# Hybrid encoder block: the low parts of the mixed Fourier channels subtracted by GpSimd in place of VectorE

## The chip, the core and the metric

The kernel runs on one NeuronCore of a Trainium2 chip. The metric is the device time of one execution in microseconds (us), lower being better; several runs are taken, and their median counts. The engines are named as in the profile: PE (TensorE matmuls), PEld (its weight loads), DVE (VectorE), ACT (ScalarE), POOL (GpSimd), SP (the queue that issues most DMAs).

## What is computed

One layer of an encoder over 2064 tokens (2048 of the sequence and 16 learned ones in front) with 1024 channels. One projection gives queries, keys and values of an attention group (4 query heads, 2 key heads) and 512 channels of a Fourier group. The part that matters here, cut from the reference:

```python
four = fourier_mix(u, w_fourier[i])     # real part of a 2-D FFT, then a 128x128 product per group
mixed = jnp.concatenate([rms_norm(attn, g_attn_out[i]), rms_norm(four, g_fourier_out[i])], axis=-1)
h = h + mixed @ w_out[i]
m = rms_norm(h, g_mlp[i])
h = h + jnp.square(jax.nn.relu(m @ w_up[i])) @ w_down[i]
```

The Fourier half of `mixed @ w_out` is the stage that is changed: `rms_norm(four)` times the lower 512 rows of `w_out`, added to `x`.

## The kernel before

Products of float32 precision are made as three fast ones. A value `a` is split into a high part `hi` (rounded to the type `fp32r`) and a low part `lo = a - hi`, and `mm3` (lines 77 to 82) issues hi x hi, hi x lo and lo x hi into one PSUM bank: L80, L81 and L82 in the profile. The helper `Split` (line 61) makes the two parts: ACT writes `hi` (L70), DVE subtracts (L71).

The kernel goes through projection, Fourier transform, attention, the two output projections and a large feed-forward part. Attention is a generator (`attention`, line 734) that is advanced in small steps by the other stages, so that its work lies among theirs. It runs in units, one for 256 queries and one key head: for each of 16 key tiles it copies scores from PSUM (`S`, ACT), takes a running maximum (`M`, DVE L779), then, one unit later, subtracts the maximum (`S`, DVE L832), takes the exponential (ACT), sums (`acc`, DVE L839), splits the result (`ph` by ACT L70, `pl` by DVE L71) and multiplies with the values (PE, tile `o`). The buffers of `ph` and `pl` are two deep.

The stage of the change is `out_f` (line 909), for 16 tiles of 128 tokens. Its function `rows(t)` (line 916) prepares tile t: the transformed channels lie in two SBUF tensors, `EV` and `UA`, with even and odd tokens apart; for each run of such tokens (128 x 4 x 64 values, one tile has its runs in two pieces) `hi` and `lo` (`yh` and `yl`, two buffers each) are written into every second column, the square goes to `sq` (`ysq`, ACT), and POOL folds the four groups of `sq` with two additions of 256 and of 128 columns:

```python
y = src[:, :, col:col + n]
o = 2 * (e - 64 * t) + par
v = slice(o, o + 2 * n - 1, 2)
split(hi[:, :, v], lo[:, :, v], y)
nc.scalar.square(sq[:, :, v], y)
```

`scale(t)` sums `sq` over the channels on PE (`pys`), takes the mean on DVE (`ms_f`, L190), and the power -1/2 on POOL (`rs_f`, L192). The products of a tile are 24 matmuls of 128x512, 12 for each half of the output channels (bank `pof`), and DVE adds `pof * rs_f` to the tokens (`xo`, L957). `rows(t + 1)` is called while the products of tile t are issued, that is one tile ahead.

The line of code says only what is done. The order in which each engine gets its instructions is made when the program is built, by a scheduler that gives every instruction a cost and puts it where it would be ready; a change of engine in one line so moves others too. Each engine then takes its instructions strictly in that order, PE included. POOL has, besides the additions and `rs_f`, the issue of the attention's loads (`q`, `kt`, `vt`, lines 711 to 744).

Of the kernel before, what the change touches and what calls it, by code (L numbers as in the profile page):

```python
# [14 lines left out]
ALU = mybir.AluOpType  # L15
# [41 lines left out]
def f32v(ap):  # L57
    return ap.bitcast(F32)
# [18 lines left out]
def mm3(nc, out, a, b, first, last, chain=False):  # L77


    nc.tensor.matmul(out, a[0], b[0], start=first, stop=False, skip_group_check=chain)  # L80
    nc.tensor.matmul(out, a[0], b[1], start=False, stop=False, skip_group_check=chain)  # L81
    nc.tensor.matmul(out, a[1], b[0], start=False, stop=last, skip_group_check=chain)  # L82
# [53 lines left out]
def encoder_block(ctx: ExitStack, tc: tile.TileContext, x, meta, w_in, w_f,  # L136
                  w_out, w_up, w_down, g_fin, g_cols, g_rows, c_id, c_rope, c_dft, c_even, c_odd, c_rem, out):
    nc = tc.nc
    split = Split(nc)
# [9 lines left out]
    def bank(name, shape=(P, 512)):  # L149
        return mmp.tile(list(shape), F32, name=name, tag="mm")  # L150
# [36 lines left out]
    def rstd_of(pool, ss, n, width, tag, rows=P):  # L187

        ms = pool.tile([P, n], F32, name="ms_" + tag, tag="ms_" + tag, bufs=2 if pool is tp else 4)
        nc.vector.tensor_scalar(ms[:rows], ss, 1.0 / width, EPS, op0=ALU.mult, op1=ALU.add)  # L190
        rs = pool.tile([P, n], F32, name="rs_" + tag, tag="rs_" + tag, bufs=2 if pool is tp else 4)
        nc.gpsimd.tensor_tensor(rs[:rows], ms[:rows], mhalf[:rows, :n], op=ALU.pow)  # L192
        return rs
# [453 lines left out]
    def y_runs(par, e0, e1):  # L647

        m, t0, o0, t1, o1 = YO if par else YE
        got = []  # L650
        if e0 < m:
            got.append((t0, o0 + e0, e0, min(e1, m) - e0))
        if e1 > m:
            s = max(e0, m)
            got.append((t1, o1 + s - m, s, e1 - s))
        return got
# [40 lines left out]
    def misc(name, shape=(P, 512)):  # L697
        return app.tile(list(shape), F32, name=name, tag="misc")
# [204 lines left out]
    def weights(pool, bufs, k, h, keep):  # L903
        raw = pool.tile([P, 512], F32, name=f"wfr{k}_{h}", tag="wr", bufs=bufs)
        nc.sync.dma_start(raw, w_out[512 + k * P:512 + (k + 1) * P, h * 512:(h + 1) * 512])
        wt[k, h] = tuple(keep.tile([P, 512], R32, name=f"wf{e}{k}_{h}") for e in "hl")
        split(*wt[k, h], raw, c_fo(k))

    def out_f():
        xts, ops = {}, {}  # L910

        def load(t):
            xts[t] = op_.tile([P, D], F32, name=f"xo_{t}", tag="xo", bufs=2)
            nc.sync.dma_start(xts[t], x[t * P:(t + 1) * P, :])

        def rows(t):

            hi = op_.tile([P, NG, P], R32, name=f"yh_{t}", tag="yh", bufs=2)
            lo = op_.tile([P, NG, P], R32, name=f"yl_{t}", tag="yl", bufs=2)
            sq = op_.tile([P, NG, P], F32, name=f"ysq_{t}", tag="ysq", bufs=2)  # L920
            for par in range(2):
                for src, col, e, n in y_runs(par, 64 * t, 64 * t + 64):
                    y = src[:, :, col:col + n]
                    o = 2 * (e - 64 * t) + par
                    v = slice(o, o + 2 * n - 1, 2)
                    split(hi[:, :, v], lo[:, :, v], y)
                    nc.scalar.square(sq[:, :, v], y)
            for n in (2, 1):
                nc.gpsimd.tensor_tensor(sq[:, :n], sq[:, :n], sq[:, n:2 * n], op=ALU.add)
            ops[t] = [hi, lo, sq]  # L930

        def scale(t):
            ps = misc(f"pys_{t}", (P, 1))
            nc.tensor.matmul(ps, ops[t].pop()[:, 0], ones, start=True, stop=True)
            ops[t].append(rstd_of(op_, ps, 1, 512, "f"))

        load(0)
        rows(0)
        for k in range(NG // 2, NG):
            for h in range(2):  # L940
                weights(wp, 3, k, h, op_)
            yield
        scale(0)
        for t in range(NT):
            hi, lo, rf = ops.pop(t)
            xt = xts.pop(t)
            for h in range(2):
                ps = bank(f"pof_{t}_{h}")
                with tc.issue_after(ended[0]) if 2 * t + h >= 2 * NT - HELD else nullcontext():
                    for k in range(NG):  # L950
                        mm3(nc, ps, (hi[:, k, :], lo[:, k, :]), wt[k, h], k == 0, k == NG - 1)
                if h == 0 and t + 1 < NT:
                    rows(t + 1)
                elif t + 1 < NT:
                    scale(t + 1)
                hs = slice(h * 512, (h + 1) * 512)
                nc.vector.scalar_tensor_tensor(xt[:, hs], ps, rf, xt[:, hs], op0=ALU.mult, op1=ALU.add)  # L957
                yield
                if h == 0 and t + 1 < NT:
                    load(t + 1)  # L960
            nc.sync.dma_start(h_d[t], xt)
# [447 lines left out]
    for g in range(8):  # L1409
# [5 lines left out]
        for name in ORDER:  # L1415
            hi, lo = ready.pop(0)
# [371 lines left out]
```

## Time and profile before

| | |
|---|---|
| median of 3 runs | 2292.0 us (2291.7 to 2292.91) |
| the profiled execution, its own time | 2293.14 us |
| its span, first to last instruction | 2291.4 us |
| granted TensorE clock, mean | 0.999 |
| PE busy | 2278.1 us (99%) |
| DVE busy | 1718.7 us (75%) |
| ACT busy | 1280.6 us (56%) |
| POOL busy | 184.0 us (8%) |
| the stage `out_f` | about 418 to 585 us of the span |

The busy times are over the whole span; the stage of the change is a fourteenth of it and has its own balance, which a view by stretches shows. A matmul's end is modelled, so two matmuls in a row overlap in the records, and a short wait of PE can hide in a longer step from one start to the next; the waits of PEld, whose loads stand ahead of the matmuls, show some of these.

### The profile page before, as it was taken

What the parts mean: (1) busy time and instruction counts of PE and PEld (TensorE: products, weight loads), DVE (VectorE), ACT (ScalarE), POOL (GpSimd) and SP (SyncE); (2) the same over time, 40 slices, a digit from 0 to 9 for tenths busy, and PEclk for the clock granted to TensorE, in tenths of its full rate; (3) what the DMA queues carried; (4) which work ended last, traced back from release to release, by engine and by line L of the source; (5) the groups of instructions that cost most, each with busy time, mean ns of one, the idle gap of its engine ahead of it and who ended that gap; (6) DMA issues with size and microseconds to landing.
All of it is one profiled execution on the core that took longest, in us unless ns stands there. A gap on an engine that the chain in (4) does not pass through costs nothing.

```text
span 2291.4 us, 30005 instructions
## 1 busy us (share of the span) xinstructions
PE 2278.1 (99%) x10846; PEld 1883.0 (82%) x10846; DVE 1718.7 (75%) x2448; ACT 1280.6 (56%) x2303; POOL 184.0 (8%) x235
## 2 busy tenths in 40 slices
PE   9999999999999999999999999999999999999998
PEld 7888988777888888888888888888888888888887
DVE  6435588999986877986887877885875656697796
ACT  6443356566665655665765775664665545543344
POOL 2212120222000000000000100000000000200000
PEclk9999999999999999999999999999999999999999
DMA  6343252543533222333342453224454444865442
GB/s 213 100 119 102 78 169 79 190 137 120 166 117 108 96 87 79 114 114 106 97 157 87 157 175 104 92 82 170 140 177 158 152 152 156 303 193 165 129 138 83
DMA packets 178069, 307.23 MB, mean 134 GB/s; under 512 B 14960, under 2 KB 63728, under 8 KB 177536
## 3 DMA queue, kind: packets, MB, share of 16 engines
q1 hardware_dynamic: 159136, 262.89, 34.9%
q0 software_dynamic: 18640, 42.16, 6.2%
q8 instruction: 85, 1.39, 0.3%
q14 instruction: 64, 0.52, 0.1%
q10 hardware_dynamic: 144, 0.26, 0.0%
HBM read 225.27 MB, written 79.99 MB: 133 GB/s over the span
## 4 chain that ended last, share of the span: by engine, by line
PE 94%; DVE 3%; DMA 1%; ACT 1%; issue 1%; POOL 0%; SPq 0%; POOLq 0%; DVEq 0%; ACTq 0%
PE pdn L80 5%; PE pdn L82 5%; PE pdn L81 5%; PE pup L80 5%; PE pup L82 5%; PE pup L81 5%; PE s L80 3%; PE s L82 3%; PE s L81 3%; PE ux L80 2%; PE ux L81 2%; PE ux L82 2%; PE dx L80 2%; PE dx L82 2%; PE dx L81 2%; PE o L81 2%
## 5 line engine op out<-in xcount | busy, mean ns | idle before, releaser
L80 PE MATMUL pdn<-wh_dn,ah 128*128 128x512 f32 x512 | 201.5, 394 | 0.2 <-ACT r L1154 0.2
L80 PE MATMUL pup<-mTh,wh_up 128*128 128x512 f32 x512 | 201.5, 394 | 0.0
L81 PE MATMUL pup<-mTl,wh_up 128*128 128x512 f32 x512 | 200.7, 392 | 0.0
L82 PE MATMUL pup<-mTh,wl_up 128*128 128x512 f32 x512 | 200.4, 391 | 0.0
L81 PE MATMUL pdn<-wl_dn,ah 128*128 128x512 f32 x512 | 199.9, 390 | 0.0
L82 PE MATMUL pdn<-wh_dn,al 128*128 128x512 f32 x512 | 198.7, 391 | 0.0
L773 ACT COPY S<-s 128x512 f32<-128x512 f32 x256 | 148.4, 584 | 55.6 <-PE s L82 48.5
L70 ACT CAST wh_up<-wr_up 128x512 fp32r<-128x512 f32 x128 | 79.4, 620 | 164.3 <-PE pup L81 76.5
L832 DVE TENSOR_TENSOR S<-S,mb 128x1024 f32<-128x1024 f32 x128 | 154.8, 1218 | 8.4 <-ACT mb L803 8.2
L71 DVE TENSOR_TENSOR pl<-S,ph 128x512 fp32r<-128x512 f32 x196 | 132.3, 696 | 11.0 <-ACT ph L70 10.7
L833 ACT ACTIVATE S<-S 128x1024 f32<-128x1024 f32 x114 | 120.7, 1060 | 34.7 <-DVE S L832 34.1
L70 ACT CAST wh_dn<-wr_dn 128x512 fp32r<-128x512 f32 x128 | 79.1, 620 | 107.9 <-PE pdn L82 52.6
L71 DVE TENSOR_TENSOR wl_up<-wr_up,wh_up 128x512 fp32r<-128x512 f32 x128 | 87.6, 687 | 68.1 <-ACT wh_up L70 63.3
L839 DVE TENSOR_TENSOR acc<-acc,S 128x1024 f32<-128x1024 f32 x110 | 134.1, 1219 | 1.3 <-ACT S L833 1.1
L71 DVE TENSOR_TENSOR wl_dn<-wr_dn,wh_dn 128x512 fp32r<-128x512 f32 x128 | 87.2, 687 | 60.2 <-ACT wh_dn L70 51.8
L70 ACT CAST ph<-S 128x512 fp32r<-128x512 f32 x196 | 118.7, 620 | 15.9 <-PE o L82 12.5
L70 ACT CAST ah<-a 128x1024 fp32r<-128x1024 f32 x56 | 58.5, 1048 | 118.2 <-issue 60.8
L779 DVE TENSOR_TENSOR M<-M,S 128x1024 f32<-128x1024 f32 x96 | 118.0, 1229 | 6.7 <-ACT S L773 6.0
L80 PEld LDWEIGHTS pdn<-wh_dn,ah 128*128 128x128 f32 x512 | 96.1, 188 | 23.5 <-ACT r L1154 3.6
L80 PE MATMUL s<-q,kt 128*128 128x512 f32 (+1 forms) x272 | 113.0, 415 | 0.1
L82 PEld LDWEIGHTS pdn<-wh_dn,al 128*128 128x128 f32 x512 | 96.2, 188 | 19.9
L82 PEld LDWEIGHTS pup<-mTh,wl_up 128*128 128x128 f32 x512 | 96.2, 188 | 19.4
(345 smaller groups left out, 6413.0 us busy)
## 6 DMA issues: line engine op xcount, KB each, us to landing
wr_up<-in_w_up_dram SPq DMA_DIRECT2D x128, 256.0 KB, 2.8
wr_dn<-in_w_down_dram SPq DMA_DIRECT2D x128, 256.0 KB, 2.6
a<-s_d SPq DMA_DIRECT2D x42, 512.0 KB, 3.6
R<-in_w_up_dram SPq DMA_DIRECT2D x16, 1024.0 KB, 5.2
s_d<-s SPq DMA_DIRECT2D x64, 256.0 KB, 2.2
d<-in_w_down_dram SPq DMA_DIRECT2D x26, 512.0 KB, 5.0
s_d<-c SPq DMA_DIRECT2D x48, 256.0 KB, 2.4
x<-in_x_dram SPq DMA_DIRECT2D x16, 512.0 KB, 4.9
```

The costliest lines, as they stand in the source:

```text
L70: self.high = nc.scalar.copy(hi, src)
L71: self.low = nc.vector.tensor_tensor(lo, src, f32v(hi), op=ALU.subtract)
L80: nc.tensor.matmul(out, a[0], b[0], start=first, stop=False, skip_group_check=chain)
L81: nc.tensor.matmul(out, a[0], b[1], start=False, stop=False, skip_group_check=chain)
L82: nc.tensor.matmul(out, a[1], b[0], start=False, stop=last, skip_group_check=chain)
L773: nc.scalar.copy(S[:, i % 2], ps)
L779: nc.vector.tensor_tensor(M, M, S, op=ALU.max)
L832: nc.vector.tensor_tensor(S, S, mb, op=ALU.subtract)
L833: nc.scalar.activation(p, S, AF.Exp, scale=ISQ)
L839: nc.vector.tensor_tensor(acc, acc, p, op=ALU.add)
```

## The change

`rows` no longer calls `split`. ACT still writes `hi`, and POOL subtracts in place of DVE:

```diff
@@ out_f, rows(t) @@
                     v = slice(o, o + 2 * n - 1, 2)
-                    split(hi[:, :, v], lo[:, :, v], y)
+                    nc.scalar.copy(hi[:, :, v], y)
+                    nc.gpsimd.tensor_tensor(lo[:, :, v], y, f32v(hi[:, :, v]), op=ALU.subtract)
                     nc.scalar.square(sq[:, :, v], y)
```

34 instructions change their engine (32 of about 256 columns, two of 12 and 16). Line numbers behind it grow by one: `xo` is L958, `pys` L935, POOL's additions L930 and its subtractions L927. On PE the order differs between the third tile of `out_f` and the first products of the stage after it, and nowhere else.

On PE, at tile 12 of `out_f` (`pof_12`), beside the last pair of key tiles of an attention unit (`o_3`, with `pl_3_15_0` and `pl_3_15_1`; `s_4` are the next unit's scores). First the place where these products now stand, as one piece of the difference:

```order
 L82 MATMUL s_4_12_5835<-q_4_5473,kt_0_1_3_4389 128x512
+L80 MATMUL o_3_5448<-ph_3_15_0_5842,vt_0_1_3_4397 128x512
+L81 MATMUL o_3_5448<-pl_3_15_0_5843,vt_0_1_3_4397 128x512
+L82 MATMUL o_3_5448<-ph_3_15_0_5842,vt_0_1_3_4397 128x512
+L80 MATMUL o_3_5448<-ph_3_15_1_5849,vt_0_1_3_4397 128x512
 L80 MATMUL s_4_13_5856<-q_4_5473,kt_0_1_3_4389 128x512
 L81 MATMUL s_4_13_5856<-q_4_5473,kt_0_1_3_4389 128x512
 L82 MATMUL s_4_13_5856<-q_4_5473,kt_0_1_3_4389 128x512
+L81 MATMUL o_3_5448<-pl_3_15_1_5850,vt_0_1_3_4397 128x512
+L82 MATMUL o_3_5448<-ph_3_15_1_5849,vt_0_1_3_4397 128x512
```

And the place where they stood:

```order
 L82 MATMUL pof_12_1_5864<-wfh2_1_4583,yl_12_5716 128x512
-L80 MATMUL o_3_5448<-ph_3_15_0_5842,vt_0_1_3_4397 128x512
 L80 MATMUL pof_12_1_5864<-wfh3_1_4603,yh_12_5715 128x512
 L81 MATMUL pof_12_1_5864<-wfl3_1_4604,yh_12_5715 128x512
 L82 MATMUL pof_12_1_5864<-wfh3_1_4603,yl_12_5716 128x512
-L81 MATMUL o_3_5448<-pl_3_15_0_5843,vt_0_1_3_4397 128x512
-L82 MATMUL o_3_5448<-ph_3_15_0_5842,vt_0_1_3_4397 128x512
-L80 MATMUL o_3_5448<-ph_3_15_1_5849,vt_0_1_3_4397 128x512
-L81 MATMUL o_3_5448<-pl_3_15_1_5850,vt_0_1_3_4397 128x512
-L82 MATMUL o_3_5448<-ph_3_15_1_5849,vt_0_1_3_4397 128x512
```

The matmul that reads `pl_3_15_0` moved up by 15 places. Others of its kind moved by 0 to 15.

On DVE, the instructions ahead of the same `pl_3_15_0`. Before:

```order
L779 TENSOR_TENSOR M_4_5593<-M_4_5593,S_4_10_5784 128x1024
L71 TENSOR_TENSOR yl_13_5822<-UA_69,yh_13_5821 128x256 x2
L832 TENSOR_TENSOR S_3_14_5344<-S_3_14_5344,mb_3_5394 128x1024
L957 SCALAR_TENSOR_TENSOR xo_12_5756<-pof_12_0_5808,rs_f_5775,xo_12_5756 128x512
L812 TENSOR_TENSOR S_3_16_5379<-S_3_16_5379,mb_3_5394 96x512
L839 TENSOR_TENSOR acc_3_5447<-acc_3_5447,S_3_14_5344 128x1024
L71 TENSOR_TENSOR pl_3_15_0_5843<-S_3_14_5344,ph_3_15_0_5842 128x512
```

Now:

```order
L71 TENSOR_TENSOR pl_3_13_1_5795<-S_3_12_5282,ph_3_13_1_5794 128x512
L779 TENSOR_TENSOR M_4_5593<-M_4_5593,S_4_10_5784 128x1024
L839 TENSOR_TENSOR acc_3_5447<-acc_3_5447,S_3_14_5344 128x1024
L71 TENSOR_TENSOR pl_3_15_0_5843<-S_3_14_5344,ph_3_15_0_5842 128x512
L958 SCALAR_TENSOR_TENSOR xo_12_5756<-pof_12_0_5808,rs_f_5775,xo_12_5756 128x512
```

Of all that stood ahead of `pl_3_15_0` since the stage began, 30 subtractions `yl` are gone and one `xo` went behind it; the rest still stands ahead, partly earlier (`S_3_14`, `S_3_16`).

On POOL, at tile 9 (the load `q_4` of the next unit's queries). Before:

```order
L929 TENSOR_TENSOR ysq_9_5412<-ysq_9_5412 128x256
L929 TENSOR_TENSOR ysq_9_5412<-ysq_9_5412 128x128
L744 DMA q_4_5473<-q_d2_104 128x2x512
L192 TENSOR_TENSOR rs_f_5372<-ms_f_5370,mhalf_100 128x1
```

Now:

```order
L930 TENSOR_TENSOR ysq_9_5412<-ysq_9_5412 128x256
L930 TENSOR_TENSOR ysq_9_5412<-ysq_9_5412 128x128
L927 TENSOR_TENSOR yl_9_5411<-UA_69,yh_9_5410 128x256 x2
L744 DMA q_4_5473<-q_d2_104 128x2x512
L192 TENSOR_TENSOR rs_f_5372<-ms_f_5370,mhalf_100 128x1
```

The two subtractions of tile 9 stand ahead of the load and of the factor `rs_f` of tile 8; at most other tiles, too, `rs_f` of a tile stands behind the subtractions of the next.

## Rows read from the trace of the kernel before

**Rows 1.** The page's first part: busy us, share of the span, instructions.

```profile
PE 2278.1 (99%) x10846; PEld 1883.0 (82%) x10846; DVE 1718.7 (75%) x2448; ACT 1280.6 (56%) x2303; POOL 184.0 (8%) x235
```

**Rows 2.** Busy time by stretches, the stage alone: columns as its first line says.

```profile
core 0: us, PE busy (x) PEld busy (x) DVE busy (x) ACT busy (x) POOL busy (x), PEclk, DMA share, GB/s
420.00:580.00 160.00, 158.50 (x707) 123.52 (x706) 153.78 (x215) 100.73 (x194) 43.34 (x54) 1.00 0.48 159
```

**Rows 3.** Waits of all engines, 410 to 590 us: total, times, longest.

```profile
PEld o L81 <- DVE pl L71: 3.3, 7, 0.8
...
PEld pm_m L787 <- DVE M L768: 1.6, 3, 0.9
```

**Rows 4.** DVE by groups, 410 to 590 us: count | busy us, mean ns | idle before.

```profile
L832 DVE TENSOR_TENSOR S<-S,mb 128x1024 f32<-128x1024 f32 x25 | 30.2, 1215 | 1.4 <-ACT mb L803 1.4
...
L779 DVE TENSOR_TENSOR M<-M,S 128x1024 f32<-128x1024 f32 x18 | 22.9, 1271 | 0.0
L71 DVE TENSOR_TENSOR pl<-S,ph 128x512 fp32r<-128x512 f32 x32 | 22.7, 740 | 0.0
L71 DVE TENSOR_TENSOR yl<-EV,yh 128x256 fp32r<-128x256 f32 x14 | 7.6, 586 | 0.1
L71 DVE TENSOR_TENSOR yl<-UA,yh 128x256 fp32r<-128x256 f32 x16 | 6.1, 415 | 0.0
L71 DVE TENSOR_TENSOR pl<-acc,ph 128x512 fp32r<-128x512 f32 x6 | 4.0, 682 | 0.0
...
L74 DVE SCALAR_TENSOR_TENSOR wfl<-wfr,cols,wfh 128x512 fp32r<-128x512 f32 x4 | 3.5, 911 | 0.0
L817 DVE TENSOR_TENSOR ph<-S,ph 32x512 fp32r<-32x512 f32 x3 | 3.1, 1048 | 0.1
L74 DVE SCALAR_TENSOR_TENSOR wl_oa<-wr_oa,cols,wh_oa 128x512 fp32r<-128x512 f32 x4 | 2.9, 737 | 0.8 <-ACT wh_oa L73 0.8
L819 DVE TENSOR_TENSOR sum<-acc 128x512 f32<-128x512 f32 x3 | 2.6, 879 | 0.1
L781 DVE TENSOR_TENSOR M<-M 128x512 f32<-128x512 f32 x3 | 2.6, 863 | 0.1
...
L71 DVE TENSOR_TENSOR yl<-UA,yh 128x12 fp32r<-128x12 f32 x1 | 0.7, 743 | 0.0
...
L71 DVE TENSOR_TENSOR yl<-UA,yh 128x16 fp32r<-128x16 f32 x1 | 0.5, 452 | 0.0
...
L71 DVE TENSOR_TENSOR yl<-EV,yh 128x244 fp32r<-128x244 f32 x1 | 0.4, 402 | 0.0
L71 DVE TENSOR_TENSOR yl<-EV,yh 128x240 fp32r<-128x240 f32 x1 | 0.4, 397 | 0.0
```

**Rows 5.** Timeline near 104 us: start, us, instruction.

```profile
103.71 0.42 DVE L420 TENSOR_TENSOR t<-qn,cg 128x256 f32<-128x256 f32 x1
...
104.26 0.80 POOL L398 TENSOR_TENSOR cg<-cs,gqk 128x256 f32<-128x256 f32 x1 [4.26 <-issue]
...
104.38 0.97 DVE L422 TENSOR_TENSOR qn<-t,t 128x256 f32<-128x256 f32 x1
```

**Rows 6.** Timeline of POOL and DVE, 549 to 562 us.

```profile
551.16 1.60 POOL L929 TENSOR_TENSOR ysq<-ysq 128x256 f32<-128x256 f32 x2 [1.03 <-ACT ysq L927]
...
551.21 2.09 DVE L71 TENSOR_TENSOR pl<-S,ph 128x512 fp32r<-128x512 f32 x2
...
558.70 1.29 DVE L71 TENSOR_TENSOR pl<-S,ph 128x512 fp32r<-128x512 f32 x2
```

**Rows 7.** Timeline of PE near 556 and 560 us.

```profile
556.00 0.39 PE L81 MATMUL s<-q,kt 128*128 128x512 f32 x1
...
559.60 0.40 PE L81 MATMUL o<-pl,vt 128*128 128x512 f32 x1
```

**Rows 8.** POOL alone: `cg` (whole span, min/median/max ns), then timeline.

```profile
L398 POOL TENSOR_TENSOR cg<-cs,gqk x34: 726/912/1195, 31.6 to 311.2; 128x256 f32<-128x256 f32 x32, 96x256 f32<-96x256 f32 x2
...
509.25 0.76 POOL L744 DMA_DIRECT2D q<-q_d  x1 [4.95 <-PE s L82]
```

**Rows 9.** Timeline of PEld near 516 us: the load that waits for `q`.

```profile
515.76 0.19 PEld L80 LDWEIGHTS s<-q,kt 128*128 128x128 f32 x1 [0.39 <-DMA q<-q_d]
```

**Rows 10.** The factor `rs_f` of tile 8 on POOL, and the `xo` that uses it.

```profile
510.03 0.61 POOL L192 TENSOR_TENSOR rs_f<-ms_f,mhalf 128x1 f32<-128x1 f32 x1
...
512.69 0.75 DVE L957 SCALAR_TENSOR_TENSOR xo<-pof,rs_f,xo 128x512 f32<-128x512 f32 x1 [1.03 <-PE pof L82]
```

## The prediction

> **What bounds the kernel.** I begin with the page's first part: PE is busy 99% of the span [rows 1]. No change of another engine can win more than PE's waiting time, and one that moves no matmul can only win or lose where PE waits. DVE is at 75% and POOL at 8%, which looks like room on both sides; but these are means over the whole span, so the next view is the stage alone. There PE is busy 158.5 of 160 us, and DVE 153.8 of 160, or 96% [rows 2]. In this stage two engines run nearly full, and POOL has 43 of 160 us filled. The reader should see that DVE is close to being the second bound here, though not in the kernel.
>
> What PE loses in the stage follows from that. Its own idle time is 160 - 158.5 = 1.5 us. The weight loads that stand ahead of the matmuls show more: 3.3 us in 7 waits for `pl`, the low part of the softmax, and 1.6 us in 3 waits for the maximum `M`, all of them for DVE [rows 3]. Part of this is hidden behind matmuls under way, so the loss of the stage lies between 1.5 and 1.5 + 4.9 = 6.4 us. This is all that any relief of DVE in this stage could give back, 0.07 to 0.28% of the time. A difference of 0.2%, that is 4.6 us, is what I take a measurement to tell from none.
>
> **What the change takes from DVE.** The six groups of `yl` add up to 7.6 + 6.1 + 0.7 + 0.5 + 0.4 + 0.4 = 15.7 us of DVE time [rows 4]. Not all of that goes away. The 16 instructions on `UA` take 415 ns, the 14 on `EV`, of the same form, 586 ns; the two small ones on `UA` take 743 and 452 ns, though they have 12 and 16 columns. Something holds them. What it is shows in the timelines: an instruction of 128x256 with two SBUF operands takes 0.42 us, and one of the same shape that starts just after an addition on POOL takes 0.97 us [rows 5]; a pair of `pl` takes 1.29 us, and 2.09 us beside a pair of `ysq` additions [rows 6]. DVE waits while POOL works. This held time belongs to the `ysq` additions, which stay, and will fall on whatever DVE runs instead. It is 14 x (586 - 415) = 2.4 us and, with 0.2 us for each small one (an estimate, below the 0.4 us of 256 columns), 0.8 us. So 15.7 - 2.4 - 0.8 = 12.5 us are really freed.
>
> **What it adds for DVE.** The same mechanism gives the price of the subtraction on POOL. A full hit by a 128x256 instruction costs DVE 0.97 - 0.42 = 0.55 us [rows 5], and a pair of 256 and 128 columns 2.09 - 1.29 = 0.80 us [rows 6]. How often a hit is full I read from the 16 pairs of `ysq` that the stage has now. Against the unheld duration of the same size [rows 4] DVE loses: `M` 18 x (1271 - 1215) = 1.0; `pl` 32 x (740 - 682) = 1.9; `yl` 2.4 + 0.8; `wfl` 4 x (911 - 737) = 0.7; `ph` 3 x (1048 - 682) = 1.1; `sum` 3 x (879 - 682) = 0.6; `M<-M` 3 x (863 - 682) = 0.5; together 9.0 us. All 16 pairs hitting fully would cost 16 x 0.80 = 12.8 us, so the share is 0.70. A new subtraction then costs DVE 0.70 x 0.55 = 0.385 us; 32 of them cost 12.3 us, and the two small ones at most 0.1 us each, an estimate. DVE gets 12.5 us back and pays 12.5 us: **the relief is nothing**, since DVE does not subtract any more but stands still while POOL does. The bounds of the price are 0 (no hit, POOL always finds DVE on PSUM operands) and 0.55 us (every one hits); a POOL instruction that takes 0.91 us, the median of `cg`, instead of 0.74 us [rows 6, 8] would add another 0.17. I take 0.385, from the nearest row: same engine, same size, same stage. Unlike the additions, the subtraction reads and writes every second column; no row shows what that costs on POOL, which keeps the upper bound open.
>
> **What the order makes of it.** The matmul work is the same. But the scheduler, as its new order shows, has counted the freed time and not the standing still: it puts the matmuls that read `pl` up to 15 places earlier. Before, they came just in time. The place that shows most is `pl_3_15_0`. DVE began that pair at 558.70 [rows 6], so the first was made at 558.70 + 0.68 = 559.4; PE read it at 559.60 [rows 7], without a wait. In the new order PE comes to it 15 places earlier, where the matmul of 556.00 stood [rows 7]. DVE has one `xo` less ahead (0.7 us) and 30 of the 34 `yl`, whose exchange is worth nothing; it makes `pl` at about 558.7. PE waits 2.7 us there. Such waits along the stage do not add up: a PE that is late by 2 us finds the next `pl` ready, so the largest one counts. Behind it, the late PE no longer waits for the last `M` of the stage (1.6 us for the three of them, so some 0.5 us) [rows 3]. The sum is 2.7 - 0.5 = **2.2 us more**. After the stage the order of PE is the same as before and PE is the bound, so nothing is made up.
>
> **What else moves, and costs nothing.** ACT's cast is the same instruction. `yl` itself is made one tile ahead of its products, and 16 tiles in some 160 us [rows 2] leave about 10 us for it; POOL needs two times 0.8 us, more where DVE holds it in turn, so PE does not wait for it. POOL's queue is the place to look at: `q_4` was issued at 509.25 [rows 8] and PE waited for it at 515.76 already [rows 9]. With the two subtractions ahead it goes out 0.5 to 2 us later, and PE waits as much longer there. By the rule that the largest wait counts, it is covered by the 2.7 us at 556 us; if that cover fails it costs up to 2 us by itself. `rs_f` of tile 8 ended at 510.64 and its `xo` began at 512.69 [rows 10]: 2 us to spare, which the two subtractions and the load nearly use.
>
> The profiled execution took 2293.1 us (span 2291.4); with the change 2295.3. The median lies 1.1 us below it, so the forecast is 2292.0 + 2.2 = **2294.2 us**.
>
> **Rivals.** (a) *No difference*, 2292.0: each 0.05 us in the price of a subtraction moves the place at 556 us by 30 x 0.05 = 1.5 us, so at 0.31 us instead of 0.385 the waits just balance. For it: the share 0.70 is read off 16 pairs, and POOL's new work comes in groups of up to four, where one hit may serve two. Against: nothing in the rows says that subtractions hit less than additions.
>
> (b) *Slower*: a hit costs the whole POOL instruction, not 0.55 us of it. Then the price is 0.70 x 0.74 = 0.52 us, the place at 556 us is 30 x 0.135 = 4.1 us later still, and the time is 2298.3. It decides from a price of 0.465 us (2.4 us over the forecast). Strided columns that made POOL's instruction longer would work in the same way: at 0.91 us a full hit is 0.72, the price 0.50 and the time 2297.7. Against the whole instruction speak rows 5, where DVE lost 0.55 us of POOL's 0.80. The Trainium skill states it in this form (SBUF — State Buffer, Who interferes with whom): a `tensor_tensor` with both inputs in SBUF contends with GpSimd's reads, and whoever comes second is blocked until the first is done. The trace agrees that there is blocking, not with its full length.
>
> (c) *Slower by the queue*: `rs_f` comes so late behind the subtractions that DVE, in its order, stands at `xo`, and all of attention's work behind it. If in half of the 16 tiles it stood 0.5 us, 4 us come on top: 2298.2. It decides from where a pair takes more than the 2 us to spare. Against: before, only the waits for PE stand ahead of `xo` [rows 10].
>
> (d) *Faster*: the subtractions mostly fall beside DVE instructions with a PSUM operand, DVE is relieved by most of 12.5 us, and PE's waits go: 1.5 to 6.4 us less, some 4, so 2288.0. It needs a price below 0.18 us. Against: every group of DVE in rows 4 works from SBUF alone, and the share of 0.70 was measured among just these neighbours.
>
> **Chances.** Forecast 0.38, (a) 0.27, (b) 0.20, (c) 0.08, (d) 0.07. Over 4.6 us slower are most of (b) and (c) and a little of the forecast's upper tail: 0.25. Over 4.6 us faster is about half of (d): 0.04. The rest, 0.71, is within 0.2%. The range goes from 2290.5 (a price of 0.25 us, and some of PE's waits gone) to 2299.5 (case (b), with the 1 us by which runs differ); it leaves out (d) and the bounds above 0.52 us.
>
> **What would show it.** Right: DVE in the stage as busy as before, within 3 us of 154 of 160, though it has 34 instructions less; `pl`, `M` and `S` on DVE with means clearly above 682 and 1215 ns; POOL near 75 us in the stage; PE waits for `pl` at L81 longer than before, the longest between 550 and 560 us. Wrong: DVE busy below 145 us and the waits of PEld for `pl` gone (case d), POOL's subtractions over 0.9 us each where nothing holds them (b), or DVE waiting for `rs_f` (c).

## The result and the profile after the change

| | kernel before | changed kernel |
|---|---|---|
| median of the runs, us | 2292.29 (16 runs, 2291.55 to 2293.67) | 2296.73 (16 runs, 2296.0 to 2298.28) |
| ratio, 95% interval | | 1.002 (1.0012 to 1.0027) |
| profiled execution, span, us | 2293.1, 2291.4 | 2297.5, 2295.7 |

The change costs 4.4 us, 0.19%. The forecast was 2294.2 us, 2.2 us more than before: the right sign, half the size.

The first part of the page of the changed kernel (busy us, share of the span, instructions), and the stage alone by stretches (columns as in [rows 2]):

```profile
PE 2279.3 (99%) x10846; PEld 1883.6 (82%) x10846; DVE 1714.5 (75%) x2414; ACT 1279.6 (56%) x2303; POOL 238.6 (10%) x269
...
420.00:580.00 160.00, 154.75 (x687) 120.45 (x686) 147.14 (x177) 97.74 (x190) 94.33 (x87) 1.00 0.44 146
```

PE's idle time in the 160 us went from 1.5 to 160 - 154.75 = 5.25 us: 3.8 us of the 4.4 are here. DVE has 34 instructions less and is busy 4.2 us less over the whole span [rows 1], so it was relieved, though not by the 15.7 us that its subtractions took [rows 4]. POOL went from 43 to 94 us in the stage.

What PE and DVE wait for in the stage, 410 to 590 us (total, times, longest), in the changed kernel:

```profile
PEld o L81 <- DVE pl L71: 7.7, 11, 1.4
...
PE o L81 <- DVE pl L71: 3.4, 6, 1.0
DVE M L779 <- ACT S L773: 3.4, 3, 1.6
PEld pm_m L787 <- DVE M L768: 2.1, 3, 1.4
...
PE pm_m L787 <- DVE M L768: 1.0, 1, 1.0
PEld pys L935 <- POOL ysq L930: 0.8, 1, 0.8
PEld s L80 <- DMA q<-q_d: 0.7, 1, 0.7
```

The waits for `pl` more than doubled (3.3 us in 7 before [rows 3]); the one for `pys`, which needs the sums of squares from POOL, is new. DVE itself now waits for `S` (line 779), which ACT copies from PE's scores: the three engines work in a loop, and what is late in one is late in the next.

DVE by groups in the same window, then POOL (count | busy us, mean ns | idle before):

```profile
L832 DVE TENSOR_TENSOR S<-S,mb 128x1024 f32<-128x1024 f32 x24 | 30.9, 1303 | 1.5 <-ACT mb L803 1.5
L839 DVE TENSOR_TENSOR acc<-acc,S 128x1024 f32<-128x1024 f32 x21 | 27.9, 1329 | 0.0
L779 DVE TENSOR_TENSOR M<-M,S 128x1024 f32<-128x1024 f32 x18 | 25.4, 1409 | 3.4 <-ACT S L773 3.4
L71 DVE TENSOR_TENSOR pl<-S,ph 128x512 fp32r<-128x512 f32 x30 | 22.9, 796 | 0.0
```

```profile
L930 POOL TENSOR_TENSOR ysq<-ysq 128x256 f32<-128x256 f32 x16 | 22.2, 1388 | 3.6 <-ACT ysq L928 3.6
...
L930 POOL TENSOR_TENSOR ysq<-ysq 128x128 f32<-128x128 f32 x16 | 17.0, 1065 | 1.1
L927 POOL TENSOR_TENSOR yl<-UA,yh 128x256 fp32r<-128x256 f32 x16 | 16.5, 1047 | 24.3 <-ACT yh L926 24.3
```

With nothing beside it DVE takes 1215 ns for 1024 columns and 682 for 512. Before, with only the additions on POOL, the means were 1271 for `M` and 740 for `pl` [rows 4]; now they are 1303 to 1409 for 1024 columns and 796 for `pl`. POOL pays as well: a subtraction takes 1047 ns in the mean, while the shortest took 745, and the additions of squares are longer than their 1015 and 740 ns of before.

How that becomes a wait of PE, at the longest one. POOL, DVE and the weight load, 554 to 561 us of the changed kernel (start, us, instruction):

```profile
554.90 1.98 POOL L927 TENSOR_TENSOR yl<-UA,yh 128x256 fp32r<-128x256 f32 x2
556.85 3.12 POOL L930 TENSOR_TENSOR ysq<-ysq 128x256 f32<-128x256 f32 x2
```

```profile
556.21 1.77 DVE L779 TENSOR_TENSOR M<-M,S 128x1024 f32<-128x1024 f32 x1
557.89 1.76 DVE L839 TENSOR_TENSOR acc<-acc,S 128x1024 f32<-128x1024 f32 x1
559.58 0.94 DVE L71 TENSOR_TENSOR pl<-S,ph 128x512 fp32r<-128x512 f32 x1
...
560.57 0.19 PEld L81 LDWEIGHTS o<-pl,vt 128*128 128x128 f32 x1 [1.40 <-DVE pl L71]
```

Two subtractions and two additions now stand in a row on POOL. `M`, `acc` and `pl`, one behind the other on DVE, lose 0.55, 0.55 and 0.26 us to them (1.22, 1.22 and 0.68 us unheld), 1.36 us in all, and PE's weight load waits 1.40 us for that `pl`. The holding does not make this wait alone: the load stands 15 places earlier than before, and the runs below show the same load in the same new order without subtractions on POOL.

### The profile page after: what moved, and what is told of

The parts are those of the page before. It is cut to its first block, busy times and chain, and to the rows that moved or that the text cites. A ratio compares the mean times of both kernels' runs of the same rounds, so it can differ in the third digit from the quotient of the medians.

```text
span 2295.7 us, 30023 instructions
## 1 busy us (share of the span) xinstructions
PE 2279.3 (99%) x10846; PEld 1883.6 (82%) x10846; DVE 1714.5 (75%) x2414; ACT 1279.6 (56%) x2303; POOL 238.6 (10%) x269
## 3 DMA queue, kind: packets, MB, share of 16 engines
q8 instruction: 85, 1.39, 0.3%
## 4 chain that ended last, share of the span: by engine, by line
PE 92%; DVE 4%; issue 1%; DMA 1%; ACT 1%; POOL 1%; POOLq 0%; DVEq 0%; SPq 0%; ACTq 0%
PE pdn L80 5%; PE pdn L82 5%; PE pdn L81 5%; PE pup L80 5%; PE pup L82 5%; PE pup L81 5%; PE dx L80 2%; PE dx L81 2%; PE dx L82 2%; PE s L80 2%; PE ux L80 2%; PE ux L81 2%; PE ux L82 2%; PE s L82 2%; PE s L81 2%; PE o L81 2%
## 5 line engine op out<-in xcount | busy, mean ns | idle before, releaser
L71 DVE TENSOR_TENSOR pl<-S,ph 128x512 fp32r<-128x512 f32 x196 | 134.1, 705 | 11.4 <-ACT ph L70 11.1
```

The lines of the kernel that those rows point to most:

```text
L71: self.low = nc.vector.tensor_tensor(lo, src, f32v(hi), op=ALU.subtract)
```

## Experiments

Three things changed together: DVE was relieved of the subtraction, POOL began to hold DVE, and the scheduler wrote another order. To part them I fixed the order. A list of instruction numbers per engine, taken from the one or the other kernel, is turned into edges that set the order of issue alone:

```
+def pin(tc):
+    info = mybir.DependencyInfo(mybir.DependencyClass.NoSync, mybir.DependencyReason.DATA)
...
+        for a, b in zip(listed, listed[1:]):
+            tc.add_manual_dep(every[b], every[a].name, info, reason="pin")
```

With it PE, DVE, ACT, SP and POOL issue everything but the subtractions in exactly the order of before ("old order") or of the change ("new order"). The subtraction then stands on DVE, on POOL, or is replaced on POOL by a fill with zeros; its own place in the order is left to the scheduler. My theory (A) at this point blamed the new order; the rival (B) the holding.

**Old order, subtraction on POOL.**

```
-                    split(hi[:, :, v], lo[:, :, v], y)
+                    nc.scalar.copy(hi[:, :, v], y)
+                    nc.gpsimd.tensor_tensor(lo[:, :, v], y, f32v(hi[:, :, v]), op=ALU.subtract)
...
         encoder_block(tc, *args)
+        pin(tc)
```

> The subtraction on GpSimd as in the changed kernel, but TensorE, VectorE, ScalarE, SyncE and GpSimd's other instructions issue the whole stage in the order of the kernel before. Theory A (the new order, planned as if the whole 15.7 us of VectorE were free, brings the waits; VectorE is in truth relieved by only some 4.5 us net): 2289 to 2292.5 us, TensorE's idle time in 420 to 580 us near the 1.5 us of before, and VectorE there near 147 us as after the change. Rival B (VectorE and GpSimd holding each other costs it, in any order): 2296 to 2297.5 us, the waits for pl and M as long as after the change.

**New order, subtraction on DVE** (the code of before, with the edges of the new order).

> The subtraction on VectorE as in the kernel before, but every engine issues the stage in the order of the changed kernel. Theory A: VectorE now lacks also the 4.5 us, so the products that come earlier wait longer: 2297 to 2303 us. Rival B: no subtraction on GpSimd, so no added holding: 2291.5 to 2293 us.

**Old order, fill**; and **new order, fill**:

```
-                    nc.gpsimd.tensor_tensor(lo[:, :, v], y, f32v(hi[:, :, v]), op=ALU.subtract)
+                    nc.gpsimd.memset(f32v(lo[:, :, v]), 0.0)
```

> Order of the kernel before on every engine; in place of the subtraction GpSimd fills the low part with zeros, which reads nothing from memory (the low part of the mixed Fourier channels is left out of the result). VectorE is then relieved of all 34 subtractions and, if an operation that reads nothing does not hold it, of their holding too. Theory A: within 1 us of the run that subtracts on GpSimd in this order, 2288 to 2292 us, since there the holding hardly counted. Rival B: 4 to 6 us below that run, 2290 to 2292 us against 2296 to 2297.5.

> Order of the changed kernel on every engine, and the fill with zeros in place of the subtraction (the low part of the mixed Fourier channels is left out of the result). Theory A in its strict form (the order alone costs it, whatever VectorE loses): 2295 to 2297 us. If it takes the order and the holding together, so that the order is good once VectorE is free as planned: 2289 to 2292 us. Rival B: 2290 to 2292 us as well; the two are told apart by the run with the subtraction on VectorE in this order.

Medians of 11 runs each in us, with the ratio to before and its interval; all four ran on one chip, where before had 2292.34:

| | on DVE | on POOL | fill on POOL |
|---|---|---|---|
| old order | 2292.34 (before) | 2295.53, 1.0015 (1.0006 to 1.0023) | 2290.71, 0.9993 (0.9984 to 1.0002) |
| new order | 2295.95, 1.0016 (1.0007 to 1.0025) | 2296.73 (the change, from its own runs) | 2291.77, 0.9996 (0.9987 to 1.0005) |

Read by rows, the subtraction on POOL costs 4.8 us over the fill in the old order, and 5.0 in the new one. I call this the holding; what the longer subtraction moves on POOL's queue is in it too. Read by columns, the new order costs 1.1 us with the fill, 1.2 with POOL and 3.6 with DVE. Taking the subtractions off DVE, with only the fill on POOL, is worth 1.6 us in the old order, where the interval includes nothing at all, and 4.2 us in the new one. An interval reaches about 2 us to either side, so the 1.1, 1.2 and 1.6 us are not sure.

The 4.4 us can thus be added up in two ways: -1.6 (relief) + 4.8 (holding) + 1.2 (order), if the order is changed last, and 3.6 (order) - 4.2 (relief) + 5.0 (holding), if it is changed first. The move to POOL alone costs 3.2 us, the new order alone 3.6, and the two together 4.4 and not 6.8: they overlap, and the share of each depends on the way taken. A alone falls, since in the old order 3.2 us of loss remain where it expected 2289 to 2292.5 us. B alone falls too: in the old order it came near (2296 to 2297.5 expected), and both fills came out as it said, but it expected 2291.5 to 2293 us from the new order with DVE. There 2295.95 us misses A's 2297 to 2303 as well.

The longest wait of the changed kernel (1.40 us, above) shows such an overlap. The same weight load in the new order with the subtractions on DVE, and under it with the fill:

```profile
558.83 0.19 PEld L81 LDWEIGHTS o<-pl,vt 128*128 128x128 f32 x1 [1.44 <-DVE pl L71]
```

```profile
555.20 0.19 PEld L81 LDWEIGHTS o<-pl,vt 128*128 128x128 f32 x1 [0.73 <-DVE pl L71]
```

At this place two subtractions on DVE delay `pl` by as much as two on POOL do, and half of the wait is there with neither, where only the additions hold `acc` and `pl`.

The first part of the page for the old order, subtraction on POOL, and under it for the fill:

```profile
PE 2279.6 (99%) x10846; PEld 1882.8 (82%) x10846; DVE 1715.6 (75%) x2414; ACT 1281.1 (56%) x2303; POOL 235.4 (10%) x269
```

```profile
PE 2276.7 (99%) x10846; PEld 1883.5 (82%) x10846; DVE 1708.4 (75%) x2414; ACT 1280.6 (56%) x2303; POOL 198.4 (9%) x269
```

Same instructions on DVE, same order: 1715.6 - 1708.4 = 7.2 us more of standing still for 34 subtractions, 0.21 us each. Against the 1718.7 of before [rows 1] DVE gained 10.3 us and gave 7.2 back. It is 3.1 us freer, and the kernel 3.2 us slower. In the new order the fill's page begins

```profile
PE 2277.3 (99%) x10846; PEld 1883.5 (82%) x10846; DVE 1711.2 (75%) x2414; ACT 1280.3 (56%) x2303; POOL 209.5 (9%) x269
```

so there the holding is 1714.5 - 1711.2 = 3.3 us of DVE, 0.10 us each, and the kernel is 5.0 us slower than with the fill. The sum of DVE's busy time does not tell what freed or held time is worth. One place where the holding becomes a wait, 476 to 484 us: DVE, POOL and PE with the subtraction, then with the fill, in the same order:

```profile
477.28 1.22 DVE L832 TENSOR_TENSOR S<-S,mb 128x1024 f32<-128x1024 f32 x1
479.34 1.56 DVE L779 TENSOR_TENSOR M<-M,S 128x1024 f32<-128x1024 f32 x1 [0.84 <-ACT S L773]
480.82 1.76 DVE L839 TENSOR_TENSOR acc<-acc,S 128x1024 f32<-128x1024 f32 x1
482.50 0.94 DVE L71 TENSOR_TENSOR pl<-S,ph 128x512 fp32r<-128x512 f32 x1
...
477.30 2.52 POOL L927 TENSOR_TENSOR yl<-EV,yh 128x256 fp32r<-128x256 f32 x2
479.79 3.11 POOL L930 TENSOR_TENSOR ysq<-ysq 128x256 f32<-128x256 f32 x2
...
483.50 0.50 PE L81 MATMUL o<-pl,vt 128*128 128x512 f32 x1 [0.96 <-DVE pl L71]
```

```profile
476.97 1.38 DVE L779 TENSOR_TENSOR M<-M,S 128x1024 f32<-128x1024 f32 x1 [0.84 <-ACT S L773]
478.27 1.21 DVE L839 TENSOR_TENSOR acc<-acc,S 128x1024 f32<-128x1024 f32 x1
479.40 0.68 DVE L71 TENSOR_TENSOR pl<-S,ph 128x512 fp32r<-128x512 f32 x1
...
475.46 1.81 POOL L930 TENSOR_TENSOR ysq<-ysq 128x256 f32<-128x256 f32 x2
...
480.14 0.50 PE L81 MATMUL o<-pl,vt 128*128 128x512 f32 x1
```

With the subtraction, POOL's additions of squares come behind it, and so fall beside `M`, `acc` and `pl`; with the fill they were over when `acc` began, PE's matmul shows no wait, and its weight load waits 0.40 us in place of 1.39 (0.80 at this place in the kernel before). The subtraction holds DVE, and it also pushes the additions, which held DVE before the change too, to where they hurt.

**Which subtractions cost.** If a few holdings that meet a wait of PE cost nearly all (theory F), a choice of tiles must show it. In the old order I put the subtraction on POOL for 4 tiles of 16, then for the other 12:

```
-                    nc.gpsimd.tensor_tensor(lo[:, :, v], y, f32v(hi[:, :, v]), op=ALU.subtract)
+                    (nc.gpsimd if t in (0, 3, 6, 13) else nc.vector).tensor_tensor(lo[:, :, v], y, f32v(hi[:, :, v]), op=ALU.subtract)
```

> Order of the kernel before on every engine; the subtraction is on GpSimd only for tiles 0, 3, 6 and 13 (8 of 34 subtractions), those beside which TensorE's new waits stood when all were there: for ysq at 425 us, for M at 451, for pl at 482 and at 555. Theory F (a few holdings that meet a wait of TensorE cost nearly all): 2294.3 to 2296 us. Rival P (each held microsecond costs the same): 8/34 of the 3.2 us, 2292.7 to 2293.6 us.

> The complement in the same order: all tiles but 0, 3, 6 and 13 on GpSimd (26 of 34 subtractions). Theory F: the holdings that mattered are gone and VectorE is still relieved, 2291 to 2292.7 us. Rival P: 26/34 of the 3.2 us, 2294.2 to 2295.4 us.

Measured: 2294.54 us, 1.001 (1.0001 to 1.0019), with 8 subtractions on POOL; 2292.92 us, 1.0004 (0.9996 to 1.0013), with the other 26; before had 2292.29 there. Eight cost 2.25 us, 26 cost 0.6: F as expected in the first, 0.2 us above its bound in the second, and P missed on both sides. Two more, with `t in (2, 5, 9, 14)` and with `t == 0`, as control and as the smallest piece:

> The control to the run with tiles 0, 3, 6 and 13: same order, as many subtractions (8), on GpSimd for tiles 2, 5, 9 and 14, beside which no new wait of TensorE stood when all were there. Theory F (it matters which holding meets a wait): 2291.7 to 2293.0 us. Rival N (any first few cost most, whichever tiles): 2294 to 2295.5 us, as for tiles 0, 3, 6 and 13.

> Same order; only tile 0's two subtractions on GpSimd, in front of tile 0's adds of squares, for whose sum TensorE came 0.8 us too early at 425 us. Theory F: this wait alone, plus 0.6 to 1.0 us: 2292.9 to 2293.4 us. Rival P (in proportion, 2 of 34): 2292.4 to 2292.6 us. The two are close to what five rounds tell apart, so the trace decides: TensorE's wait for ysq at 425 us is there or not.

Measured, with before at 2292.06: 2292.59 us, 1.0001 (0.9992 to 1.001), for the control, so eight other subtractions cost nothing that can be measured; 2293.0 us, 1.0004 (0.9995 to 1.0013), for tile 0, whose interval includes nothing, so the trace has to decide. Waits of the weight loads, 410 to 590 us, with tiles 0, 3, 6 and 13, then the control, then tile 0 alone:

```profile
PEld o L81 <- DVE pl L71: 4.6, 7, 1.2
PEld pm_m L787 <- DVE M L768: 2.0, 3, 1.3
...
PEld pys L935 <- POOL ysq L930: 0.8, 1, 0.8
```

```profile
PEld o L81 <- DVE pl L71: 2.9, 7, 0.8
PEld pm_m L787 <- DVE M L768: 1.6, 3, 0.9
```

```profile
PEld pys L935 <- POOL ysq L930: 0.8, 1, 0.8
```

The control has no wait that before did not have [rows 3]. Tile 0 alone brings the wait for `ysq`: its two subtractions stand ahead of its own additions on POOL, and PE's weight load waits 0.8 us. So of the 2.25 us of the eight some 0.9, going by the medians, come by POOL's own queue and not by a held `pl` or `M`. By how much the `xo` of a place (line 957 before, 958 now) starts later than in the kernel before, in us, read from the timelines:

```
at (kernel before)        430.5   450.3   463.3   481.2   521.8   580.7
tiles 0, 3, 6, 13         +0.70   +1.41   +2.39   +2.84   +3.29   +3.20
tile 0                    +0.68   +0.88   +0.86   +0.93   +1.21   +0.96
tiles 2, 5, 9, 14         -0.05   -0.05   -0.08   -0.25   -0.17   -0.71
```

The delays add up, step by step, and none is made good by the next. (The traced execution of the first of these took 2296.1 us, 1.6 more than its median, so its last figures are larger than the 2.25 us.)

**Both engines subtract.** In the old order DVE makes the low part as before, and POOL the same again behind it:

```
                     split(hi[:, :, v], lo[:, :, v], y)
+                    nc.gpsimd.tensor_tensor(lo[:, :, v], y, f32v(hi[:, :, v]), op=ALU.subtract)
```

> Order of the kernel before; VectorE makes the low part as before, and GpSimd makes the same again behind it, so VectorE is held as in the changed kernel and not relieved of anything. If holding and relief add up (holding +4.8 us, from the difference between subtraction and fill in this order; relief -1.6 us): 2296.4 to 2298 us. If the cost came from the low part being made later or from GpSimd's own queue, and not from VectorE being held: 2292 to 2293.5 us.

Measured: 2303.71 us (5 runs), 1.0049 (1.0036 to 1.0061), 11.4 us more than before, outside both expectations. The page's first part and the stage alone:

```profile
PE 2279.8 (99%) x10846; PEld 1882.5 (82%) x10846; DVE 1727.8 (75%) x2448; ACT 1281.0 (56%) x2303; POOL 233.3 (10%) x269
...
420.00:580.00 160.00, 150.89 (x663) 116.06 (x662) 154.83 (x203) 95.05 (x185) 88.36 (x86) 1.00 0.42 142
```

DVE's whole time rose by 9.1 us, about the 7.2 of the other pair of runs; but the kernel lost 11.4 us and not 4.8. So holding and relief don't add up. My reading is that with the subtractions still on DVE, which was at 153.8 of 160 us [rows 2], the 9 us have no room; no run tests it. A part is not holding at all, but POOL's queue, since its copy of the work waits for DVE's: PE's wait for `pys` grew as follows (PE, 424 to 432 us).

```profile
426.62 0.38 PE L935 MATMUL pys<-ones,ysq 128*128 128x1 f32 x2 [2.22 <-POOL ysq L930]
```

How much of the 11.4 us is the one and how much the other this run doesn't part.

**One input in place of two.** Old order, POOL copies `y` into the low part:

```
-                    nc.gpsimd.tensor_tensor(lo[:, :, v], y, f32v(hi[:, :, v]), op=ALU.subtract)
+                    nc.gpsimd.tensor_copy(lo[:, :, v], y)
```

> Order of the kernel before; GpSimd copies y into the low part in place of subtracting (one input in place of two; the low part of the result is wrong by that, so its value is left out of the output). If only operations with two inputs hold VectorE, as the fill held nothing: 2290 to 2291.5 us and VectorE's group means as in the run with the fill. If every reading of memory by GpSimd holds it: 2293 to 2295.5 us, with xo, pl and M longer as with the subtraction.

Measured: 2291.39 us, 0.9996 (0.9987 to 1.0005), with before at 2292.29, inside the first expectation. First part of its page, and two POOL groups, 410 to 590 us:

```profile
PE 2276.8 (99%) x10846; PEld 1883.2 (82%) x10846; DVE 1707.5 (75%) x2414; ACT 1280.3 (56%) x2303; POOL 217.7 (10%) x269
...
L927 POOL CAST yl<-UA 128x256 fp32r<-128x256 f32 x16 | 13.5, 874 | 20.9 <-PE pof L82 20.9
L927 POOL CAST yl<-EV 128x256 fp32r<-128x256 f32 x14 | 10.6, 779 | 13.3 <-PE py L81 8.0 <-PE pof L82 5.3
```

DVE is busy 1707.5 us, as with the fill (1708.4): the copy holds DVE by nothing that shows. One reservation holds for copy and fill: they don't wait for `yh` on ACT, so POOL begins them earlier (the idle time ahead ends with PE here, and with ACT's `yh` in the changed kernel), and they meet other DVE instructions than the subtraction does.

## Why the prediction was right, and where its size was wrong

- *PE is the bound, and the change can only act where PE waits.* Right. 3.8 of the 4.4 us are PE's idle time in the stage.
- *DVE is freed of 12.5 us.* About right: with the fill DVE's whole time is 10.3 us below before.
- *A subtraction costs DVE 0.385 us; relief nothing.* The mechanism was right and the size too high: 0.21 us in the old order, 7.2 us for 34, and 0.10 us in the new one. The full hit of 0.55 us is there as forecast (`M` and `acc` at 556 us). The share of full hits is smaller than the 0.70 read from the additions, probably because a subtraction often follows or precedes another POOL instruction that meets the same long DVE instruction; I did not test that. DVE was in truth relieved by 4.2 us.
- *So the time in itself doesn't change.* This step failed, as a sum: it set held time against freed time as if a microsecond of each were worth the same. By it, the 4.2 us by which DVE came out freer should have brought a gain on the way to rival (d). In the old order, with no help from the scheduler, the time rose by 3.2 us. In the new order the exchange cost 0.8 us (2296.73 against 2295.95), near the forecast's nothing, but as the difference of 5.0 held and 4.2 freed, which the sum did not have. What is freed is worth what PE waits for there: 1.6 us in the old order, where the scheduler had put the subtractions in places where PE hardly waited, and 4.2 us in the new one. What is held lies where POOL happens to work: eight subtractions met the chain of `M`, `acc` and `pl`, or the sums of squares, ahead of a matmul, and cost 2.25 us; eight others cost nothing that could be measured.
- *The new order adds 2.2 us, by one wait of 2.7 us at 556 us.* That the new order costs time is shown where DVE still subtracts: 3.6 us. With POOL or fill it is 1.1 to 1.2 us, less than the intervals tell apart. The longest wait stands where the forecast had it, at 559 to 561 us with what had been lost till then, and the exchange is worth nothing there, as forecast; but it is 1.4 us instead of 2.7, and it is one of many.
- *Waits don't add up, the largest one counts.* Wrong, and as far as the waits tell the reason why the forecast had half of the cost: the weight loads' waits for `pl` rose from 3.3 us in 7 [rows 3] to 7.7 in 11, though the longest is 1.4. The steps of +0.70, +1.41, +2.39 and +2.84 us in the table add up, step by step. As I read it, a late PE makes ACT's `S` late, and with it the next `M` and `pl` on DVE; the 3.4 us for which DVE waits for `S` in the changed kernel fit that, but no run tested it by itself.
- *POOL near 75 us, `yl` in time, `rs_f` in time.* POOL had 94 us, since DVE holds it in turn. DVE had 147.1 us in the stage, not within 3 us of 154, so that sign of the prediction failed. PE never waited for `yl`, and DVE not for `rs_f` in the changed kernel, so rival (c) did not happen there. In the old order the profile puts 1.2 us of DVE's wait at `xo` down to `yl` on POOL and 0.5 us to `rs_f`, once each. The wait for `q_4` grew from 0.4 us [rows 9] to 0.7 only. The queue did cost elsewhere: 0.8 us at `pys`, which the prediction had not looked at.
- *Rival (b), a hit costs the whole POOL instruction.* It came nearer to the time (2298.3) than the forecast, by a reason that did not hold: 0.55 us remained the full hit, and strided columns cost POOL next to nothing (745 ns at the shortest, against 726 for `cg`, which has no stride [rows 8]). The Trainium skill (SBUF — State Buffer, Who interferes with whom) calls the port pair that the two engines share "an exclusive lock", and says that a `tensor_tensor` with both inputs in SBUF contends with GpSimd's reads. The runs agree on blocking, in both directions, and show less than the whole instruction: 0.55 us of at least 0.745.
- *The time.* The sign was right, for the reason given (PE comes too early for `pl`) and for one that the sum had put at nothing (the exchange, in the old order). That the time fell inside the range is partly luck: one wait was taken too long, the others were left out, and the range's upper end came from (b), whose reason did not hold.

No version here beats the kernel before by more than a measurement can tell. The fill in the old order is the lowest: with the subtraction gone from both engines, 1.6 us are won at the median.

## What to carry to other kernels

In a loop that one engine closes at 99%, don't set freed time against held time: where the scheduler has laid the work of the second engine into its gaps, freeing it buys little (1.6 us here), while standing still falls anywhere, and the part that falls ahead of a wait adds up with the others. Look at which instruction of the second engine the third one will meet, and whether a POOL burst of several two-input instructions stands ahead of something that TensorE reads. Fix the order before you blame the scheduler for a difference, and measure the new order with the old work too: here the order alone cost 3.6 us, the move alone 3.2, and both together 4.4, so that neither has a share of its own.

## What the hardware showed unasked

- The holding goes both ways. A subtraction of 745 ns on POOL took 1047 in the mean, and up to 5.3 us in the old order, where DVE, itself not held, ran `pl`, `M`, `acc` and the like one behind the other:

```profile
L927 POOL TENSOR_TENSOR yl<-UA,yh x18: 223/754/5299, 494.0 to 573.5; 128x256 fp32r<-128x256 f32 x16, 128x12 fp32r<-128x12 f32 x1, 128x16 fp32r<-128x16 f32 x1
```

- A copy with one input on POOL is held too (424 ns at the median, 3834 at the longest) but hardly held DVE here (whole time 1707.5 us, 1708.4 with the fill):

```profile
L927 POOL CAST yl<-UA x18: 195/424/3834, 491.0 to 569.0; 128x256 fp32r<-128x256 f32 x16, 128x12 fp32r<-128x12 f32 x1, 128x16 fp32r<-128x16 f32 x1
```

- A fill on POOL, which reads nothing, takes 333 ns for 128x256 and is not held (the two of 240 and 244 columns took 326 and 325):

```profile
L927 POOL MEMSET yl<- 128x256 f32 x30 | 9.0, 333 | 34.6 <-PE pof L82 26.6 <-PE py L81 8.0
```
